# Five buffers for gathered rows instead of three in the last stage of a 46,509-instruction block kernel

## The chip, the cores and the metric

The kernel runs on one core of a Trainium2 chip. TensorE (PE) multiplies, VectorE (DVE) and ScalarE (ACT) work elementwise, GpSimd (POOL) does some elementwise work and issues the indirect transfers (gathers), SyncE (SP) issues the plain transfers. The engines run side by side, each in its own fixed order. The metric is the device time of one execution in microseconds (us).

## The reference

Two transformer blocks over 256 tokens of width 2048, in float32. The stage that is changed is the last: the second half of a feed-forward layer with a lookup (PEER). Each token has 8 x 16 = 128 chosen experts out of 16,384, each with a weight; the layer's output is the weighted sum of the experts' rows of `peer_v`. A residual is added, and a last norm is applied.

```python
a = einsum('cd,ced->ce', xc, u[ic])            # stage U: token times chosen rows of peer_u
w = gelu(a) * gate
y = einsum('ce,ced->cd', w, v[ic])             # stage V: weighted sum of chosen rows of peer_v
x = x + y
out = rms_norm_2(x, g_final)
```

## The kernel before, in words

The two tables (16,384 rows of 2048 columns each) are worked on in two ways. For the first columns (`GU` = 640 of `peer_u`, `GV` = 512 of `peer_v`) the chosen rows are gathered, one per token: a gather fetches 128 rows, the s-th expert of 128 tokens. For the other columns the whole table is streamed and multiplied densely, with a matrix of weights `L` (tokens by experts, zero where an expert was not chosen).

Stage V runs over 128 blocks of 128 experts. In a block, SP loads three raw tiles of 128 x 512 (`vraw`, six slots). Each is split for TensorE into a high and a low part: ScalarE writes `vh` (L210), VectorE writes `vl` (L212), six slots each. The weights are split in the same way (`wh`, `wl`), once per two blocks. Then TensorE makes 18 matmuls of 128 x 512, three (L1520, L1525, L1526) for each of three column groups `n` and two token halves `tt`, into six accumulators `va`.

Beside it run 256 gathers (2 token halves times 128 slots) of 128 x 512 into tiles `gt`. `gather` (L1261) has GpSimd issue the indirect transfer, and `add` (L1473) has VectorE multiply the gathered rows by their weight and add them into `y` (L1474). A list `flying` holds up to three gathers; a new one goes into the buffer that the oldest add has freed. Each block takes `n` adds, the rest divided by the blocks left up to 126:

```python
n = -(-left // max(NE - 2 - i, 1)) if i else 0
```

Two loads of residual rows (`load_y`) and the five parts of the last norm's vector (`gfin`) are queued on SP behind the last raw tile of blocks 1, 16 and 24. In the last two blocks the matmuls are ordered by hand: those of block 126 are held back and then sorted by token half, so that the first half's accumulators are done while the second half's are still worked on; the first half's norm runs beside them. After the last matmul come the final sums, the norm's products (GpSimd mostly), the scaling and the stores.

The order of each engine's work is laid out ahead of time by a planner that goes through the program in order of priority, with its own costs for each instruction; `keep_in_program_order` keeps an add behind all VectorE work that was written before it, while work written later may be moved ahead of it. Tiles of a pool with one tag share its slots, and an instruction that would write to a slot waits until the earlier readers are done.

Stage U, ahead of V, has the same shape: gathers of 128 x 640 with five buffers (four of `BASE`, one of `EXTRA`) beside a streamed part whose raw tiles hold 704 KB.

Of the kernel before, what the change touches and what calls it, by code (L numbers as in the profile page):

```python
# [12 lines left out]
F32 = mybir.dt.float32  # L13
F32R = mybir.dt.float32r
# [6 lines left out]
P = 128  # L21
T = 256
NT = 2
D = 2048
KD = D // P
W = 512
DFF = 8192
EPS = 1e-6
GU = 640
GV = 512  # L30
# [23 lines left out]
def tile_conv_mlp_then_attention_peer(ctx, tc, a, out):  # L54
    nc = tc.nc
    PSUM = bass.MemoryType.PSUM
# [643 lines left out]
    with ExitStack() as pc:  # L700
# [310 lines left out]
        with ExitStack() as pj:  # L1011
# [6 lines left out]
            for n, src in enumerate((so, lo_)):  # L1018
                c = 0
# [47 lines left out]
    NE = 128  # L1067
# [144 lines left out]
    ready = []  # L1212
# [45 lines left out]
    EXTRA = {"gt": 1, "u": 1}  # L1258
    UNITS = [(k, min(4, KU - k)) for k in range(0, KU, 4)]

    def gather(pool, bufs, w, table, tt, s):  # L1261
        gt = pool.tile([P, w], F32, name="gt", tag="gt", bufs=bufs)
        nc.gpsimd.indirect_dma_start(  # L1263
            out=gt, out_offset=None, in_=table,
            in_offset=bass.IndirectOffsetOnAxis(ap=e4[:, tt, s:s + 1], axis=0),
        )
        return gt, tt, s
# [18 lines left out]
    for i in range(NE):  # L1286
        if i == len(HALVES):
            eb_ctx.close()
            own["gt"] = us_ctx.enter_context(tc.tile_pool(name="ug", bufs=2))
        if more is None and not bg.items and "gt" in own:  # L1290
            rt_ctx.close()
            rt_ctx = ExitStack()
            more = rt_ctx.enter_context(tc.tile_pool(name="more", bufs=2, side=side))
        if i % 2 == 0:
            aps = psa.tile([P, 2, T], F32, name="aps", tag="acc")
        if i in HALVES:
            ready_parts = []
            for n in range(2):
                t = (us, eb)[i % 2].tile([P, KU, P], F32, name="ue", tag="uraw")
                nc.sync.dma_start(  # L1300
                    t.rearrange("p k e -> p (k e)"),
                    pre.done[i][n].rearrange("p k e -> p (k e)"),
                )
                ready_parts.append(t.bitcast(F32R))
        else:
            raw = us.tile([P, DU], F32, name="uraw", tag="uraw")
            if i in pre.done:
                nc.sync.dma_start(raw, pre.done[i][0].rearrange("p k e -> p (k e)"))
                rawt = raw.rearrange("p (k e) -> p k e", k=KU)
            else:  # L1310
                nc.sync.dma_start(raw, a["peer_u_2"][0, i * P:(i + 1) * P, GU:D])
                rawp = raw.rearrange("p (j k) -> p k j", k=KU)
        for k0, nk in UNITS:
            if i in HALVES:
                hi_k = [ready_parts[0][:, k0 + kk, :] for kk in range(nk)]
                lo_k = [ready_parts[1][:, k0 + kk, :] for kk in range(nk)]
            else:
                pool = ring("u")
                nb = EXTRA["u"] if pool is more else BASE["u"]
                uh = pool.tile([P, 4, P], F32R, name="uh", tag="uh", bufs=nb)  # L1320
                ul = pool.tile([P, 4, P], F32R, name="ul", tag="ul", bufs=nb)
                if i in pre.done:
                    split(uh[:, :nk], ul[:, :nk], rawt[:, k0:k0 + nk])
                else:
                    with tc.high_priority(offset=EARLY):
                        ut = pst.tile([P, 4, P], F32, name="tp_u", tag="tr")
                        for kk in range(nk):
                            nc.tensor.transpose(ut[:, kk, :], rawp[:, k0 + kk, :], ident)  # L1328
                    split(uh[:, :nk], ul[:, :nk], ut[:, :nk])
                hi_k = [uh[:, kk, :] for kk in range(nk)]  # L1330
                lo_k = [ul[:, kk, :] for kk in range(nk)]
            for kk in range(nk):
                k = k0 + kk
                s0, s1 = k == 0, k == KU - 1
                o = aps[:, i % 2, :]
                nc.tensor.matmul(o, lhsT=hi_k[kk], rhs=xbh[:, k, :], start=s0, stop=False)  # L1336
                nc.tensor.matmul(o, lhsT=hi_k[kk], rhs=xbl[:, k, :], start=False, stop=False)  # L1337
                nc.tensor.matmul(o, lhsT=lo_k[kk], rhs=xbh[:, k, :], start=False, stop=s1)  # L1338
            bg.pump(1)
        if i % 2 == 1:  # L1340
            nc.scalar.activation(
                L[:, :, i - 1:i + 1], aps.rearrange("p i t -> p t i"), AF.Copy
            )
        n = min(len(ready) + len(flying), -(-left // (NE - i))) if more is not None else 0
        for _ in range(n):
            while ready and len(flying) < BASE["gt"] + EXTRA["gt"]:
                pool = ring("gt")
                nb = EXTRA["gt"] if pool is more else BASE["gt"]
                flying.append(gather(pool, nb, GU, u4, *ready.pop(0)))
            dot(*flying.pop(0))  # L1350
        left -= n
    us_ctx.close()
# [99 lines left out]
    ps_ctx.close()  # L1452


    with tc.tile_pool(name="psv", bufs=1, space=PSUM) as psv, tc.tile_pool(name="vs", bufs=2) as vs:
        NV = DN // W
        H = W // 2
        ys = [
            xb_pool.tile([P, D + W + H], F32, name=f"y{tt}", tag=("xbh", "xbl")[tt]) for tt in range(NT)
        ]  # L1460
        gl = vs.tile([P, W], F32, name="gl", bufs=1)
        gfin = [
            (0, W, ys[0][:, D:D + W]), (W, 2 * W, ys[1][:, D:D + W]), (2 * W, 3 * W, gl),
            (3 * W, 3 * W + H, ys[0][:, D + W:]), (3 * W + H, D, ys[1][:, D + W:]),
        ]

        def load_y(lo, hi):
            for tt in range(NT):
# [4 lines left out]
        def add(gt, tt, s):  # L1473
            tc.keep_in_program_order(nc.vector.scalar_tensor_tensor(  # L1474
                ys[tt][:, 0:GV], gt, wtok[:, tt, s:s + 1], ys[tt][:, 0:GV], ALU.mult, ALU.add
            ))

        vslots = [(tt, s) for tt in range(NT) for s in range(SL)]
        left = len(vslots)
        for i in range(NE):  # L1480
# [6 lines left out]
                    split(wh[:, :, ts], wl[:, :, ts], L[:, ts, i:i + 2].rearrange("p t i -> p i t"))  # L1487
            vhl = []
            for n in range(NV):
                raw = vr.tile([P, W], F32, name="vraw", tag="vraw")  # L1490
                fetch = nc.sync.dma_start(
                    raw, a["peer_v_2"][0, i * P:(i + 1) * P, GV + n * W:GV + (n + 1) * W]
                )
                vh = vs.tile([P, W], F32R, name="vh", tag="vh", bufs=6)
                vl = vs.tile([P, W], F32R, name="vl", tag="vl", bufs=6)
                op = split(vh, vl, raw)
                vhl.append((vh, vl))
            with tc.issue_after(fetch.ins):
                if i == 1:
                    load_y(0, GV)  # L1500
                elif i == 16:
                    load_y(GV, D)
                elif i == 24:
                    for lo, hi, g_ in gfin:
                        nc.sync.dma_start(g_, bcast_row(a["g_final_2"][lo:hi], hi - lo))
            if i == 8:
# [4 lines left out]
            if i == 0:  # L1511
                todo.sort(key=lambda c: c[2])
            if i == NE - 2:
                held, todo = todo, []
            elif i == NE - 1:
                todo = sorted(held + todo, key=lambda c: (c[2], c[1], c[0]))
            for e, n, tt, (vh, vl) in todo:
# [6 lines left out]
                    tc.keep_in_program_order(op)  # L1524
                nc.tensor.matmul(acc[tt][n], lhsT=wh[:, e % 2, tk], rhs=vl, start=False, stop=False)  # L1525
                nc.tensor.matmul(acc[tt][n], lhsT=wl[:, e % 2, tk], rhs=vh, start=False, stop=s1)  # L1526
            n = -(-left // max(NE - 2 - i, 1)) if i else 0
            for _ in range(min(n, left)):
                while vslots and len(flying) < 3:
                    flying.append(gather(vs, 3, GV, v4, *vslots.pop(0)))  # L1530
                add(*flying.pop(0))
                left -= 1

        for tt in range(NT):
            y = ys[tt]
            part = sm.tile([P, 4], F32, name="fp", tag="ssq4")
            for c in range(4):
                cs = slice(c * W, (c + 1) * W)
                if c:
                    nc.vector.tensor_tensor(y[:, cs], acc[tt][c - 1], y[:, cs], ALU.add)  # L1540
                junk = vs.tile([P, W], F32, name="fj", tag="gt", bufs=3)
                nc.scalar.activation(junk, y[:, cs], AF.Square, accum_out=part[:, c:c + 1])
                mul = nc.vector if (tt, c) == (1, 3) else nc.gpsimd
                for lo, hi, g_ in gfin:
                    if c * W <= lo < (c + 1) * W:
                        mul.tensor_tensor(y[:, lo:hi], y[:, lo:hi], g_, ALU.mult)
            ssq = sm.tile([P, 1], F32, name="fssq", tag="ssq")
            nc.vector.tensor_reduce(ssq, part, AX.X, ALU.add)
            rr, _ = rms_scale(ssq, D, f"fin{tt}")
            w = 2 * W if tt == 0 else W  # L1550
            for c in range(D // w):
                cs = slice(c * w, (c + 1) * w)
                if tt == 1 and c % 2:
                    nc.scalar.activation(y[:, cs], y[:, cs], AF.Copy, scale=rr)
                else:
                    nc.vector.tensor_scalar(y[:, cs], y[:, cs], rr, None, ALU.mult)
                nc.sync.dma_start(out[0, tt * P:(tt + 1) * P, cs], y[:, cs])
# [18 lines left out]
```

## Time and profile before

| | |
|---|---|
| median of 3 runs | 3219.36 us (3219.32 to 3228.66) |
| the profiled execution | 3219.82 us |
| its span in the profile | 3218.1 us |
| mean granted TensorE clock | 0.989 of full |
| TensorE, VectorE, ScalarE, GpSimd busy | 3067.6, 2382.2, 1573.3, 862.3 us |
| data moved | 799.51 MB, mean 248 GB/s |
| stage V, first to last matmul starts | 2600.0 to 3204.6 us |

Times in the rows are in us from the span's start unless marked ns. A group's row gives the line, the engine, the operation, the tiles written and read, and the count. Idle time is put down to what ended it. Matmuls are pipelined, so their busy times overlap. The chain of waits is followed back from the last instruction, at each step to what released it.

### The profile page before, as it was taken

The page shows a single profiled execution, that of the slowest core. Times are in us where ns is not written, and L with a number is a line of the kernel's source. Part 1 is how long each engine was busy: PE and PEld are TensorE (multiplying, and loading weights), DVE is VectorE, ACT ScalarE, POOL GpSimd, SP SyncE. Part 2 cuts the span into 40 slices and gives each one's busy share as a digit, 9 for nine tenths or more (in the row PEclk, how much of TensorE's full clock was granted, in tenths as well). Part 3 has the DMA queues.
Part 4 walks back from the last instruction along what each step waited for, and adds up shares of the span by engine and source line. Part 5 has one row for each costly group of instructions (what it writes and reads, how often), then busy time and mean ns, then how long its engine had stood idle before and what let it go on. Part 6 is the DMA issues. An engine that isn't in the chain of part 4 may idle for free.

```text
span 3218.1 us, 46509 instructions
## 1 busy us (share of the span) xinstructions
PE 3067.6 (95%) x16266; PEld 2571.2 (80%) x16266; DVE 2382.2 (74%) x4415; ACT 1573.3 (49%) x2574; POOL 862.3 (27%) x823
## 2 busy tenths in 40 slices
PE   8889999999999999999999989999999998889997
PEld 7668777787888877777788889999998976667775
DVE  6987677666777765455777977776777977778887
ACT  7555555444454465545445223334443564445554
POOL 1640000000000000000000016654444964555554
PEclk9999999999999999999999999999999999999999
DMA  6445599998999844445997479998886358888886
GB/s 212 134 167 185 179 298 314 317 300 257 306 312 314 265 156 154 157 163 170 318 300 254 160 248 323 333 313 288 283 287 209 122 196 296 279 269 293 293 281 233
DMA packets 334502, 799.51 MB, mean 248 GB/s; under 512 B 29143, under 2 KB 67002, under 8 KB 334010
## 3 DMA queue, kind: packets, MB, share of 16 engines
q1 hardware_dynamic: 273744, 574.82, 54.7%
q0 software_dynamic: 52192, 207.26, 19.0%
q10 hardware_dynamic: 8330, 14.44, 1.3%
q8 instruction: 128, 2.10, 0.3%
q14 instruction: 108, 0.88, 0.1%
HBM read 731.66 MB, written 64.75 MB: 247 GB/s over the span
## 4 chain that ended last, share of the span: by engine, by line
PE 59%; DMA 21%; DVE 9%; issue 8%; POOL 2%; ACT 1%; SPq 0%; DVEq 0%; ACTq 0%; POOLq 0%
PE acc L378 13%; PE acc L379 13%; PE acc L380 13%; DMA gt<-peer_v,e 12%; PE aps L1338 4%; PE aps L1336 4%; PE aps L1337 4%; DVE gc L522 2%; PE tp_u L1328 2%; PE ep L1406 2%; PE wp L1437 1%; DVE lo L212 1%; POOL gt L1263 1%; DVE y L1474 1%; DMA uraw<-peer_u 1%
## 5 line engine op out<-in xcount | busy, mean ns | idle before, releaser
L212 DVE TENSOR_TENSOR lo<-raw,hi 128x1024 fp32r<-128x1024 f32 (+2 forms) x580 | 707.5, 1229 | 361.2 <-ACT hi L210 359.5
L210 ACT ACTIVATE hi<-raw 128x1024 fp32r<-128x1024 f32 (+2 forms) x580 | 605.0, 1049 | 559.4 <-PE acc L380 432.1
L379 PE MATMUL acc<-lo,xbh 128*128 128x512 f32 (+1 forms) x1034 | 414.6, 401 | 15.2 <-DVE lo L212 15.1
L380 PE MATMUL acc<-hi,xbl 128*128 128x512 f32 (+1 forms) x1034 | 412.8, 400 | 0.0
L378 PE MATMUL acc<-hi,xbh 128*128 128x512 f32 (+1 forms) x1034 | 409.0, 400 | 0.9 <-ACT hi L210 0.9
L1263 POOL DMA_INDIRECT gt<-peer_u,e x256 | 282.6, 1104 | 467.8 <-DVE gt L1270 206.7
L1263 POOL DMA_INDIRECT gt<-peer_v,e x256 | 305.6, 1194 | 290.5 <-DVE y L1474 255.7
L210 ACT ACTIVATE vh<-vraw 128x512 fp32r<-128x512 f32 x384 | 239.6, 633 | 289.0 <-DMA vraw<-peer_v 233.0
L1338 PE MATMUL aps<-xbh,ul 128*128 128x256 f32 x1254 | 365.1, 291 | 5.8 <-DVE ul L212 5.6
L1336 PE MATMUL aps<-xbh,uh 128*128 128x256 f32 x1254 | 363.1, 290 | 0.0
L1337 PE MATMUL aps<-xbl,uh 128*128 128x256 f32 x1254 | 360.8, 288 | 0.0
L1525 PE MATMUL va<-vl,wh 128*128 128x512 f32 x768 | 313.1, 408 | 46.7 <-DVE vl L212 45.9
L1526 PE MATMUL va<-vh,wl 128*128 128x512 f32 x768 | 300.9, 392 | 0.0
L1520 PE MATMUL va<-vh,wh 128*128 128x512 f32 x768 | 297.7, 393 | 2.7 <-ACT vh L210 2.6
L1474 DVE SCALAR_TENSOR_TENSOR y<-gt,wtok,y 128x512 f32<-128x512 f32 x256 | 191.9, 749 | 115.2 <-DMA gt<-peer_v,e 113.7
L212 DVE TENSOR_TENSOR vl<-vraw,vh 128x512 fp32r<-128x512 f32 x384 | 255.9, 685 | 4.6 <-ACT vh L210 4.6
L1338 PEld LDWEIGHTS aps<-xbh,ul 128*128 128x128 f32 x1254 | 241.1, 192 | 10.8 <-DVE ul L212 10.7
L379 PEld LDWEIGHTS acc<-lo,xbh 128*128 128x128 f32 x1034 | 196.5, 190 | 66.4 <-DVE lo L212 20.9
L1336 PEld LDWEIGHTS aps<-xbh,uh 128*128 128x128 f32 x1254 | 241.0, 192 | 0.6
L1337 PEld LDWEIGHTS aps<-xbl,uh 128*128 128x128 f32 x1254 | 240.9, 192 | 0.0
L1525 PEld LDWEIGHTS va<-vl,wh 128*128 128x128 f32 x768 | 144.8, 188 | 119.7 <-DVE vl L212 91.6
L378 PEld LDWEIGHTS acc<-hi,xbh 128*128 128x128 f32 x1034 | 196.8, 190 | 48.2 <-ACT hi L210 2.1
(549 smaller groups left out, 6297.0 us busy)
## 6 DMA issues: line engine op xcount, KB each, us to landing
vraw<-peer_v SPq DMA_DIRECT2D x384, 256.0 KB, 4.8
raw<-w_in SPq DMA_DIRECT2D x88, 1024.0 KB, 5.0
raw<-w_up SPq DMA_DIRECT2D x64, 1024.0 KB, 8.2
raw<-w_down SPq DMA_DIRECT2D x64, 1024.0 KB, 7.1
uraw<-peer_u SPq DMA_DIRECT2D x64, 704.0 KB, 5.7
uraw<-ud SPq DMA_DIRECT2D x50, 704.0 KB, 5.8
tq<-peer_u SPq DMA_DIRECT2D x152, 176.0 KB, 7.3
ud<-tu POOLq DMA_DIRECT2D x38, 704.0 KB, 6.7
```

The source lines that it names most:

```text
L210: op = nc.scalar.activation(hi, src, AF.Copy, scale=scale)
L212: nc.vector.tensor_tensor(lo, src, hi, ALU.subtract)
L378: nc.tensor.matmul(o, lhsT=xh_, rhs=hi, start=s0, stop=False)
L379: nc.tensor.matmul(o, lhsT=xh_, rhs=lo, start=False, stop=False)
L380: nc.tensor.matmul(o, lhsT=xl_, rhs=hi, start=False, stop=s1)
L1263: nc.gpsimd.indirect_dma_start(out=gt, out_offset=None, in_=table, in_offset=bass.IndirectOffsetOnAxis(ap=e4[:, tt, s:s + 1], axis=0),)
L1336: nc.tensor.matmul(o, lhsT=hi_k[kk], rhs=xbh[:, k, :], start=s0, stop=False)
L1337: nc.tensor.matmul(o, lhsT=hi_k[kk], rhs=xbl[:, k, :], start=False, stop=False)
L1338: nc.tensor.matmul(o, lhsT=lo_k[kk], rhs=xbh[:, k, :], start=False, stop=s1)
L1520: op = nc.tensor.matmul(acc[tt][n], lhsT=wh[:, e % 2, tk], rhs=vh, start=s0, stop=False)
L1525: nc.tensor.matmul(acc[tt][n], lhsT=wh[:, e % 2, tk], rhs=vl, start=False, stop=False)
L1526: nc.tensor.matmul(acc[tt][n], lhsT=wl[:, e % 2, tk], rhs=vh, start=False, stop=s1)
```

## The change

Five things in stage V. (1) The gathers go into five tiles `gts`, used in turn by hand, instead of three slots of a tag; up to five fly. (2) The raw tiles get a seventh slot, in a pool of its own; the split tiles have five slots each instead of six. (3) The adds are spread over the blocks up to 120 instead of 126. (4) The last norm's vector is loaded at block 123 (`NE - 5`) instead of 24; its third part goes into the first gather tile instead of a tile of its own, and the scratch tile of the norm's squares takes three of the gather tiles in turn. (5) Of block 126 only the matmuls of column groups 1 and 2 are held back for the last block; those of group 0 run at once.

```diff
-    def gather(pool, bufs, w, table, tt, s):
-        gt = pool.tile([P, w], F32, name="gt", tag="gt", bufs=bufs)
+    def gather(gt, table, tt, s):
...
-                flying.append(gather(pool, nb, GU, u4, *ready.pop(0)))
+                gt = pool.tile([P, GU], F32, name="gt", tag="gt", bufs=nb)
+                flying.append(gather(gt, u4, *ready.pop(0)))
...
-    with tc.tile_pool(name="psv", bufs=1, space=PSUM) as psv, tc.tile_pool(name="vs", bufs=2) as vs:
+    with tc.tile_pool(name="psv", bufs=1, space=PSUM) as psv, ExitStack() as vs_ctx:
+        vs = vs_ctx.enter_context(tc.tile_pool(name="vs", bufs=2))
...
-        gl = vs.tile([P, W], F32, name="gl", bufs=1)
+        gts = [vs.tile([P, GV], F32, name=f"gt{n}", bufs=1) for n in range(5)]
         gfin = [
-            (0, W, ys[0][:, D:D + W]), (W, 2 * W, ys[1][:, D:D + W]), (2 * W, 3 * W, gl),
+            (0, W, ys[0][:, D:D + W]), (W, 2 * W, ys[1][:, D:D + W]), (2 * W, 3 * W, gts[0]),
             (3 * W, 3 * W + H, ys[0][:, D + W:]), (3 * W + H, D, ys[1][:, D + W:]),
         ]
+        gnext = 0
...
+        v2 = vs_ctx.enter_context(tc.tile_pool(name="v2", bufs=1))
+        vturn = 0
...
-                raw = vr.tile([P, W], F32, name="vraw", tag="vraw")
+                raw = (vr if vturn % 7 < 6 else v2).tile([P, W], F32, name="vraw", tag="vraw")
+                vturn += 1
...
-                vh = vs.tile([P, W], F32R, name="vh", tag="vh", bufs=6)
-                vl = vs.tile([P, W], F32R, name="vl", tag="vl", bufs=6)
+                vh = vs.tile([P, W], F32R, name="vh", tag="vh", bufs=5)
+                vl = vs.tile([P, W], F32R, name="vl", tag="vl", bufs=5)
...
-                elif i == 24:
+                elif i == NE - 5:
                     for lo, hi, g_ in gfin:
                         nc.sync.dma_start(g_, bcast_row(a["g_final_2"][lo:hi], hi - lo))
...
             if i == NE - 2:
-                held, todo = todo, []
+                held = [c for c in todo if c[1]]
+                todo = [c for c in todo if not c[1]]
...
-            n = -(-left // max(NE - 2 - i, 1)) if i else 0
+            n = -(-left // max(NE - 8 - i, 1)) if i else 0
             for _ in range(min(n, left)):
-                while vslots and len(flying) < 3:
-                    flying.append(gather(vs, 3, GV, v4, *vslots.pop(0)))
+                while vslots and len(flying) < len(gts):
+                    flying.append(gather(gts[gnext], v4, *vslots.pop(0)))
+                    gnext = (gnext + 1) % len(gts)
                 add(*flying.pop(0))
                 left -= 1
...
-                junk = vs.tile([P, W], F32, name="fj", tag="gt", bufs=3)
+                junk = gts[1 + c % 3]
```

## Rows read from the trace of the kernel before

**Rows 1.** the page's chain that ended last, share of the span by line

```profile
PE acc L378 13%; PE acc L379 13%; PE acc L380 13%; DMA gt<-peer_v,e 12%; PE aps L1338 4%; PE aps L1336 4%; PE aps L1337 4%; DVE gc L522 2%; PE tp_u L1328 2%; PE ep L1406 2%; PE wp L1437 1%; DVE lo L212 1%; POOL gt L1263 1%; DVE y L1474 1%; 
```

**Rows 2.** matmuls into va in stage V: duration min/median/max ns, first and last start

```profile
L1520 PE MATMUL va<-vh,wh x768: 387/389/632, 2600.0 to 3204.1; 128*128 128x512 f32 x192
...
L1526 PE MATMUL va<-vh,wl x768: 387/389/632, 2601.1 to 3204.6; 128*128 128x512 f32 x192
```

**Rows 3.** TensorE at the end of stage V, first and last of 25

```profile
3199.09 0.40 PE L1526 MATMUL va<-vh,wl 128*128 128x512 f32 x1
...
3204.55 0.39 PE L1526 MATMUL va<-vh,wl 128*128 128x512 f32 x1
```

**Rows 4.** stage V: us, PE, PEld, DVE, ACT, POOL, PEclk, DMA share, GB/s

```profile
2600.00:3205.00 605.00, 557.56 (x2304) 424.91 (x2304) 481.89 (x714) 307.76 (x464) 310.93 (x261) 0.99 0.85 280
```

**Rows 5.** the chain of waits from 2580 us on, by line

```profile
by line: DMA gt<-peer_v,e 58.8%; issue 13.5%; DVE y L1474 6.5%; DVE vl L212 4.5%; DMA vraw<-peer_v 3.4%; POOL gt L1263 3.1%; PE va L1525 1.5%; PE va L1526 1.3%; PE va L1520 1.2%; PE wp L1437 1.0%; DVE wl L212 0.9%; PE ep L1406 0.6%; ACT vh 
```

**Rows 6.** waits in stage V: engine, line, waited for: us in total, times, longest

```profile
ACT vh L210 <- DMA vraw<-peer_v: 233.0, 197, 6.3
DVE y L1474 <- DMA gt<-peer_v,e: 113.7, 126, 3.6
...
PE va L1525 <- DVE vl L212: 45.9, 61, 2.6
ACT vh L210 <- PE va L1526: 23.1, 18, 3.8
```

**Rows 7.** timeline of stage V: start, us, engine, line, operation [idle before <-releaser]

```profile
2942.27 1.15 POOL L1263 DMA_INDIRECT gt<-peer_v,e  x1 [0.71 <-DVE y L1474]
...
2949.00 1.29 DVE L212 TENSOR_TENSOR vl<-vraw,vh 128x512 fp32r<-128x512 f32 x2
...
2949.35 1.15 POOL L1263 DMA_INDIRECT gt<-peer_v,e  x1 [1.01 <-DVE y L1474]
...
2950.20 0.75 DVE L1474 SCALAR_TENSOR_TENSOR y<-gt,wtok,y 128x512 f32<-128x512 f32 x1
...
2950.87 0.69 DVE L212 TENSOR_TENSOR vl<-vraw,vh 128x512 fp32r<-128x512 f32 x1
...
2952.91 1.07 DVE L212 TENSOR_TENSOR wl<-L,wh 128x512 fp32r<-128x512 f32 x1
...
2953.89 0.68 DVE L212 TENSOR_TENSOR vl<-vraw,vh 128x512 fp32r<-128x512 f32 x1
```

**Rows 8.** the adds in stage V: duration ns, first and last start

```profile
L1474 DVE SCALAR_TENSOR_TENSOR y<-gt,wtok,y x256: 731/751/757, 2603.6 to 3194.7; 128x512 f32<-128x512 f32 x128
```

**Rows 9.** DMA of stage V: packets, MB, share; KB each, median to landing

```profile
q1 hardware_dynamic: 55584, 102.00, 50.3%
q0 software_dynamic: 20480, 67.13, 34.3%
...
gt<-peer_v,e POOLq DMA_INDIRECT x256, 5.5
y<-res_d SPq DMA_DIRECT2D x2, 768.0 KB, 8.9
```

**Rows 10.** a stretch of stage U, columns as in rows 4

```profile
1940.00:2140.00 200.00, 194.23 (x1547) 188.63 (x1547) 157.74 (x347) 73.50 (x139) 122.80 (x114) 1.00 0.93 333
```

**Rows 11.** DMA issues in that stretch, columns as in rows 9

```profile
uraw<-peer_u SPq DMA_DIRECT2D x22, 704.0 KB, 6.9
uraw<-ud SPq DMA_DIRECT2D x17, 704.0 KB, 6.0
gt<-peer_u,e POOLq DMA_INDIRECT x114, 6.5
```

**Rows 12.** transfers of raw tiles in stage V

```profile
DMA to landing us min/median/max: 2.5/4.8/8.1
```

**Rows 13.** VectorE in the tail

```profile
3206.59 1.00 DVE L176 TENSOR_TENSOR rms_y<-rms_y,rms_t 128x1 f32<-128x1 f32 x1
```

## The prediction

> **What bounds the kernel now.** I read the page first. Its chain of waits is mostly TensorE in the projections, but one transfer has 12% of the span, the gathered rows of peer_v [rows 1]. They belong to the last stage, V, which the change alone touches, so the rest is read there. V runs from its first matmul at 2600.0 us to its last at 3204.55 + 0.39 = 3204.9 us [rows 2, 3], 604.9 us, and in it no engine is full: VectorE is busy 482 of 605 us, GpSimd 311, ScalarE 308, the DMA engines 0.85 [rows 4]. TensorE's 558 us are pipelined matmuls that overlap, so I use its dense pace: from 3199.09 to 3204.55 us 24 matmuls start, 0.2275 us each [rows 3]. All 2304 would take 524 us, and a block (18) 4.10. TensorE therefore lacks work for about 80 us.
>
> What it lacks is split rows, and what those lack stands in the chain of V: 58.8% is "gather lands", 3.4% raw rows [rows 5]. The waits give it in time: VectorE stands 113.7 us in 126 waits for a gather at the add (L1474), and TensorE 45.9 us for the low half of a split, which VectorE makes [rows 6]. VectorE is in order: while it stands at an add, the splits behind it wait, raw slots stay taken, ScalarE waits for raw rows (233 us), and TensorE runs dry. So the wait for raw rows is mostly a result.
>
> Why is a gather late? There are three buffers. GpSimd issues one at 2942.27; when it has landed, its add frees the buffer, and the gather three further on, into the same buffer, goes out at 2949.35 [rows 7]. 7.08 us for three is 2.36 us per row, and 256 such are 604 us: the stage's length. The adds do take from 2603.6 to 3194.7 us, 2.31 us each [rows 8]. V runs at the pace of the gather loop.
>
> **The change, part by part.** Costs per block at full pace, for the next bounds:
> - TensorE: 4.10 us.
> - VectorE, by starts of neighbours [rows 7]: a split 0.605 (two end after 1.29, one alone is 0.685), an add 0.67, a weight split 0.98, one per two blocks. With two adds 1.815 + 0.49 + 1.34 = 3.65 us, with three 4.32, with none 2.31.
> - DMA: the two data queues took 50.3 + 34.3% of 16 engines for 606 us to move 169.1 MB [rows 9], so full engines need 3.03 us per MB. Three raw tiles (0.786 MB) and two gathers (0.524) take 3.97 us, with three gathers 4.77, with none 2.38.
>
> *Five gather buffers.* The loop becomes five per turn. If the turn stays 7.08 us, that is 1.42 us a gather; the nearest row for a fuller DMA is the U stage with its five buffers: 114 gathers in 200 us, 1.75 us each, of 2.5 KB rows [rows 10, 11]. Those are the ends; at two adds per block they ask for 2.8 to 3.5 us, under TensorE's 4.10, so the loop ceases to bind there. GpSimd's own 1.15 us per issue [rows 7], 2.3 to 3.5 us per block, hides beside it.
>
> A rule of the Trainium skill speaks against this part. The profile's median from issue to landing is 5.5 us [rows 9]. "DMA: Bandwidth & Descriptors", section Anatomy of one DMA, gives about 2.0 us fixed and bytes/436 GB/s beside it, which for 256 KB is an estimated 2.6 us. By it the old loop would turn in some 4.2 us (the trace's 7.08 less 5.5, and 2.6), three buffers would give a row per 1.4 us, and this part would be worth nothing; the 126 waits say otherwise.
>
> *Adds finish six blocks earlier.* The divisor goes from 126 - i to 120 - i. Worked through the loop: before, 6 blocks have three adds and 119 have two; after, blocks 1 to 18 have three, 19 to 119 two, the last eight none. The first 18 blocks thus ask for 4.77 us of DMA, and 4.25 to 5.25 of the gather loop (three times the ends above): they are slower than TensorE. I take the DMA at the share 0.96, between the U stage's 0.93 [rows 10] and full: 4.97 us.
>
> *Seven raw slots.* A raw slot's turn is landing (median 4.8 us [rows 12]) plus some 2.5 us of issue, split and queue, against 7 x 1.365 = 9.6 us of TensorE time for seven tiles. It gives 1.4 us more cover; by itself zero, it keeps a fuller DMA from showing.
>
> *Five split slots.* One tile less ahead, 1.37 us. ScalarE stood 18 times because all were full [rows 6], at most 18 x 1.37 = 25 us; at least nothing, since four tiles (5.5 us) still lie ahead. It matters only where VectorE is late too, which is 61 of the 768 matmuls that take it [rows 2, 6], 8%: 2 us.
>
> *The last norm's vector.* Its five loads (1.05 MB, 3.2 us of DMA) move from block 24, where DMA is wanted, to block 123, where no gather runs. In SP's queue they stand behind that block's raw load and ahead of the later ones; one goes into the first gather buffer, which the last gather also uses. Its add belongs to block 119, and that raw load already waits for a split of block 121, so SP should stop nowhere: zero. If the add were late, SP would hold the raw rows of four blocks for that time, some 2 us. The 3.2 us are inside the bounds per block.
>
> *Holding two of three column groups.* Block 126's first group is now multiplied at once, so only five tiles need be held. The last token half keeps 15 matmuls rather than 18, 0.7 us less cover for the first half's norm. Against it, the first column's products on GpSimd are done early; in the trace, the last of its 1.3 us products lie beside VectorE's tiny norm steps, which take 1.00 us and delay the final sums [rows 13]. Between -1.3 and +0.7: -0.5 us.
>
> **The sum for V.** Block 0: 4.1. 18 blocks at 4.97: 89.5. The residual rows at block 16, 1.57 MB [rows 9], DMA-bound: 5.0. 101 blocks: TensorE and DMA are 4.10 and 3.97, so close that they disturb one another; the U stage in that state kept TensorE busy 194.2 of 200 us [rows 10], 0.97: 4.22 each, 426.2. Eight at 4.10: 32.8. Split slots: 2. Together 559.6, that is 45.3 less than 604.9; with the tail 45.8. The profiled run took 3219.8 us (span 3218.1), the runs' median 3219.4, so they are one: **3174 us**.
>
> Range: with full engines, 18 at 4.77 and 109 at TensorE's pace, V is 542 us (3156); nothing but TensorE, 524 (3139). With a DMA share of 0.90, blocks at 5.30 and 4.41, it is 583 (3198); with the split slots at half their worst about 3210. I put 3148 to 3208.
>
> **The rivals.**
> - *Raw rows become late: slower.* V's transfers share engines that are 0.85 busy; two more gathers in flight stand before each raw tile. If the raw slot's turn exceeds 7 x 604.9 / 384 = 11.0 us, V is slower than before; with 2.5 us around it, that means landing over 8.5 us, where now it is 4.8 at the median and 8.1 at most [rows 12]. At 9 us, 11.5 / 7 = 1.64 us per tile: 631 us, 3246. Against it: in the U stage five gathers fly beside 704 KB tiles and these land in 6 to 6.9 us [rows 11]. The Trainium skill's front page, "Trainium Kernel Development and Optimization", Key Constraints, says the same of the engines: all queues run on the same 16 and interleave. The share in this trace leaves 15% to interleave into. 7 in 100.
> - *Gathers slow in proportion.* If the gather path itself gives 2.3 us per row whatever the depth, five in flight take 11.8 us each and V stays: 3219. The U stage's 1.75 us for larger rows [rows 11] speaks against it. With it goes the case that the loop does not bind at all and VectorE stands at the adds for another reason, which also leaves 3219; the turn of 7.08 us, which gives the stage's length by itself, speaks against that. Together 8 in 100. The rule on the fixed cost, above, would make it this case.
> - *DMA holds it short.* Share near 0.90 or the first 18 blocks at the loop's worst: 3190 to 3210, about 3200; 20 in 100. Before, the share in V was 0.85 [rows 4], which speaks for it.
> - *TensorE alone.* DMA and VectorE leave no gaps: below 3156, about 3148. VectorE's 3.65 of 4.10 us leaves little slack; 10 in 100.
>
> The forecast itself (3156 to 3190) has 55 in 100. A measurement of this kernel tells 0.3%, 9.7 us, from no change. Faster by more takes the forecast, the short case and TensorE alone: 0.85; same 0.08; slower 0.07.
>
> **What would show it.** After: the waits of the add for gathers fall from 113.7 us to under 40, mostly in the first 18 blocks, which should take some 90 us; the chain of V leaves the gather for TensorE and splits; the DMA share in the middle is 0.93 to 0.97; gathers land in 6 to 7 us and raw rows in 5 to 6.5; the last matmul stands near 3159 us; GpSimd issues its last gather some 40 us before that. The prediction is wrong if raw rows land over 8.5 us, if the order that the planner gives VectorE puts adds ahead of splits that TensorE needs, or if SP stands at the vector's loads.

## The result, and the profile after

The changed kernel takes 3142.1 us (median of 6 runs, 3134.8 to 3156.9) against 3221.6 us for the kernel before on the same chips: 0.9751 of it, 95% interval 0.9731 to 0.9771. The gain of 79.5 us is well over the forecast 45, and the time lies 6 us below the stated range.

The profiled execution has a span of 3142.2 us, 75.9 less than before. Its first and last groups of V's matmuls (columns as in [rows 2]):

```profile
L1526 PE MATMUL va<-vh,wh x768: 387/389/794, 2601.9 to 3128.0; 128*128 128x512 f32 x192
...
L1532 PE MATMUL va<-vh,wl x768: 388/389/628, 2603.4 to 3128.5; 128*128 128x512 f32 x192
```

V runs from 2601.9 to 3128.5 + 0.4 = 3128.9 us, 527.0 us instead of 604.9. It begins 1.9 us later, and from its end to the span's end there are 13.3 us, before 13.2. So -77.9 + 1.9 + 0.1 = -75.9: all of it is V.

The chain of V, by line, which [rows 5] shows for before:

```profile
by line: PE va L1531 19.9%; PE va L1526 19.9%; PE va L1532 19.8%; issue 9.5%; POOL gt L1262 6.4%; DMA gt<-peer_v,e 5.8%; DMA vraw<-peer_v 5.3%; DVE y L1476 2.7%; DVE vl L212 2.5%; PE wp L1437 1.2%; PE ep L1406 1.0%; ACT oj L1428 0.8%; DVE w
```

Three shares of 20% are TensorE's own matmuls; the gather's landing has gone from 58.8% to 5.8%. The waits, as in [rows 6]:

```profile
ACT vh L210 <- PE va L1532: 153.6, 195, 3.1
...
ACT vh L210 <- DMA vraw<-peer_v: 18.7, 23, 1.9
...
DVE y L1476 <- DMA gt<-peer_v,e: 7.7, 7, 4.0
...
PE va L1531 <- DVE vl L212: 1.6, 1, 1.6
```

They have turned round. TensorE waits 1.6 us for a low half (45.9 before), the add 7.7 us for gathers (113.7). ScalarE now waits for TensorE to free a split slot, 153.6 us: the queue ahead of TensorE is full. Raw rows, 233 us of waiting before, are at 18.7. The seventh slot is not what did that: with five gather tiles and six raw slots (below) they are at 32.8, which bears out that most of that wait was a result of VectorE's stops.

V in stretches of 40 us (columns as in [rows 4]):

```profile
2600.00:2640.00 40.00, 38.13 (x162) 31.39 (x163) 35.92 (x54) 26.72 (x42) 27.02 (x23) 0.96 0.95 319
2640.00:2680.00 40.00, 39.55 (x174) 32.19 (x173) 35.95 (x55) 21.64 (x33) 24.85 (x23) 1.00 1.00 363
2680.00:2720.00 40.00, 40.00 (x178) 32.95 (x177) 38.34 (x59) 23.44 (x36) 26.60 (x22) 1.00 0.98 337
...
2800.00:2840.00 40.00, 38.41 (x170) 31.50 (x169) 35.53 (x54) 22.32 (x33) 31.63 (x22) 1.00 0.95 319
2840.00:2880.00 40.00, 40.00 (x178) 33.14 (x177) 39.80 (x61) 23.92 (x35) 30.09 (x25) 1.00 1.01 363
...
2960.00:3000.00 40.00, 40.00 (x178) 33.10 (x178) 36.92 (x55) 23.44 (x35) 23.95 (x21) 1.00 0.95 321
```

At TensorE's dense pace 40 us hold 176 matmuls, and those that overlap an edge are counted too, so 178 is a stretch without a gap. Only the first two and the sixth fall short. The DMA share is 0.95 to 1.01 up to 3080 us, where the gathers end.

The two data queues and the issues (columns as in [rows 9]):

```profile
q1 hardware_dynamic: 55728, 102.26, 55.3%
q0 software_dynamic: 20480, 67.13, 37.4%
...
vraw<-peer_v SPq DMA_DIRECT2D x378, 256.0 KB, 5.3
gt<-peer_v,e POOLq DMA_INDIRECT x256, 6.0
```

Gathers land in 6.0 us at the median (5.5 before), raw rows in 5.3 (4.8).

### The profile page after: what moved, and what is told of

It is laid out like the page before. It is cut to its first block, busy times and chain, and to the rows that moved or that the text cites. A ratio compares the mean times of both kernels' runs of the same rounds, so it can differ in the third digit from the quotient of the medians.

```text
span 3142.2 us, 46502 instructions
## 1 busy us (share of the span) xinstructions
PE 3034.4 (97%) x16266; PEld 2575.7 (82%) x16266; DVE 2380.8 (76%) x4415; ACT 1570.3 (50%) x2574; POOL 870.8 (28%) x823
## 4 chain that ended last, share of the span: by engine, by line
PE 71%; DMA 11%; DVE 8%; issue 6%; POOL 2%; ACT 2%; SPq 0%; ACTq 0%; POOLq 0%; DVEq 0%
PE acc L378 13%; PE acc L379 13%; PE acc L380 13%; PE aps L1337 4%; PE aps L1335 4%; PE aps L1336 4%; PE va L1531 4%; PE va L1526 4%; PE va L1532 4%; DMA uraw<-peer_u 2%; DVE gc L522 2%; PE tp_u L1327 2%; POOL gt L1262 2%; PE ep L1406 2%; PE wp L1437 1%
## 5 line engine op out<-in xcount | busy, mean ns | idle before, releaser
L1262 POOL DMA_INDIRECT gt<-peer_v,e x256 | 321.0, 1254 | 169.4 <-DVE y L1476 111.4
L210 ACT ACTIVATE vh<-vraw 128x512 fp32r<-128x512 f32 x384 | 236.1, 632 | 191.7 <-PE va L1532 153.6
L1531 PE MATMUL va<-vl,wh 128*128 128x512 f32 x768 | 299.3, 390 | 1.6 <-DVE vl L212 1.6
L380 PEld LDWEIGHTS acc<-hi,xbl 128*128 128x128 f32 x1034 | 195.7, 189 | 46.1 <-issue 2.3
L1526 PE MATMUL va<-vh,wh 128*128 128x512 f32 x768 | 226.5, 391 | 2.5 <-ACT vh L210 2.5
L1269 DVE SCALAR_TENSOR_TENSOR gt<-gt,xg 128x640 f32<-128x640 f32 x256 | 203.3, 820 | 21.0 <-DMA gt<-peer_u,e 20.4
```

What stands on the lines that cost most here:

```text
L210: op = nc.scalar.activation(hi, src, AF.Copy, scale=scale)
L380: nc.tensor.matmul(o, lhsT=xl_, rhs=hi, start=False, stop=s1)
L1262: nc.gpsimd.indirect_dma_start(out=gt, out_offset=None, in_=table, in_offset=bass.IndirectOffsetOnAxis(ap=e4[:, tt, s:s + 1], axis=0),)
L1526: op = nc.tensor.matmul(acc[tt][n], lhsT=wh[:, e % 2, tk], rhs=vh, start=s0, stop=False)
```

## The experiments

All are variants of the changed kernel. The chips differ by some 20 us, so each has the ratio to the kernel before on its own chip, and the length of V in its one profiled execution (first matmul to last). The changed kernel: 0.9751 and 527.0 us, and in a second measurement below 0.9743 and 524.6, so V differs by 2.4 us between two executions of one kernel.

**Three gather tiles.**

```diff
-        gts = [vs.tile([P, GV], F32, name=f"gt{n}", bufs=1) for n in range(5)]
+        gts = [vs.tile([P, GV], F32, name=f"gt{n}", bufs=1) for n in range(3)]
...
-                junk = gts[1 + c % 3]
+                junk = vs.tile([P, W], F32, name="fj", tag="fj", bufs=2)
```

> The changed kernel with three gather tiles again, all else kept. If the gather loop was the bound (7.1 us for three rows, some 7.5 with the fuller queues), 256 adds take 605 to 640 us and the kernel about 3215 to 3250 us. If the raw slots, the later vector or the spread of the adds brought the gain, it stays near 3142.

Measured: 1.0089 (1.0059 to 1.0118), as much as 3250 us on the chips of the result, V 634.8 us. The whole gain is gone, and a little more. The adds, and who waits up to 3130 us (as in [rows 8] and [rows 6]):

```profile
L1476 DVE SCALAR_TENSOR_TENSOR y<-gt,wtok,y x256: 732/751/764, 2625.4 to 3218.4; 128x512 f32<-128x512 f32 x128
```

```profile
DVE y L1476 <- DMA gt<-peer_v,e: 106.6, 104, 3.4
...
PE va L1531 <- DVE vl L212: 57.0, 66, 2.2
```

To the end of V the two waits come to 132.9 and 67.3 us (113.7 and 45.9 before). The adds take 593.0 us, 2.32 each, as in the kernel before and a little under the 605 expected, although seven raw slots and all other parts of the change are there. Since they must end at block 120 now, the eight blocks left come on top: from the last add at 3218.4 to the end of the last matmul at 3251.7 are 33.3 us, eight times 4.16, where the kernel before has 10.2. With three tiles the earlier end of the adds thus makes up 23 of the 30 us by which V is longer than before; another 5 are a later first add.

**Four gather tiles.** The same line with `range(4)`.

> Four gather tiles. By the loop, 7.1 to 7.6 us for four is 1.8 to 1.9 us a row, 454 to 486 us for 256, below TensorE's 524: 3142 to 3155 us. If the pace is simply in proportion to the tiles, or the planner's order asks for more, it lands half way, near 3170.

Measured: 0.9763 (0.9741 to 0.9784), V 539.3 us. The loop's arithmetic holds: four are nearly enough. The add still waits 31 us for gathers in the profile; whether the fifth tile is worth the 12 us that V shows is not settled by the times, whose interval overlaps with the changed kernel's.

**Five gather tiles alone.** The change pays for them with the sixth split slots, so this keeps what pays for them.

```diff
-                raw = (vr if vturn % 7 < 6 else v2).tile([P, W], F32, name="vraw", tag="vraw")
+                raw = vr.tile([P, W], F32, name="vraw", tag="vraw")
...
-            (0, W, ys[0][:, D:D + W]), (W, 2 * W, ys[1][:, D:D + W]), (2 * W, 3 * W, gts[0]),
+            (0, W, ys[0][:, D:D + W]), (W, 2 * W, ys[1][:, D:D + W]), (2 * W, 3 * W, gl),
...
-                elif i == NE - 5:
+                elif i == 24:
...
-            n = -(-left // max(NE - 8 - i, 1)) if i else 0
+            n = -(-left // max(NE - 2 - i, 1)) if i else 0
```

> The kernel before with five gather tiles alone, and what makes room for them (five split slots, one column group of block 126 not held back); six raw slots, adds up to block 126, the vector at block 24. If the loop is the whole cause: 3140 to 3150 us. If the seventh raw slot is needed beside it, raw rows are waited for again: 3160 to 3185.

Measured: 0.9758 (0.9738 to 0.9779), V 535.4 us. The gather tiles, with the five split slots and the group of block 126 that isn't held back, bring practically all of the gain in time, and 69.5 of the 77.9 us of V. No add waits for a gather any more, and raw rows are waited for (as in [rows 6], up to 3130 us):

```profile
ACT vh L210 <- DMA vraw<-peer_v: 32.8, 32, 4.9
```

**Six raw slots.** Only the first edit of the five gather tiles alone, the one above.

> The changed kernel with six raw slots instead of seven. If raw rows land in 5 to 6 us, a slot's turn of about 8 us is just the 8.2 us that TensorE takes for six tiles: 3142 to 3152 us. If the seventh slot carries part of the gain: 3160 or more.

Measured: 0.9774 (0.9748 to 0.9799), V 540.0 us; the interval overlaps with the changed kernel's, so it was run again beside it (below).

**Adds up to block 126.** Only the last edit of the five gather tiles alone. The gathers that come after block 123 overwrite the third part of the norm's vector in the tile that they share, so columns 1024 to 1535 are scaled with the wrong gain; the instructions are the same.

> The changed kernel with the adds spread up to block 126 as before. If TensorE alone sets the pace, 3140 to 3147 us. If ending the adds early is part of the gain (the last blocks free of gathers, the first column's norm early), 3150 or more.

Measured: 0.9754 (0.9727 to 0.9781), V 529.0 us: no difference. The early end of the adds brings no time; it makes the shared tile possible.

**Three adds in each of the first 18 blocks, enforced.** The planner may move splits of later blocks ahead of an add. This forbids it in blocks 2 to 19:

```diff
-                op = split(vh, vl, raw)
+                op = nc.scalar.activation(vh, raw, AF.Copy)
+                low = nc.vector.tensor_tensor(vl, raw, vh, ALU.subtract)
+                if 2 <= i <= 19:
+                    tc.keep_in_program_order(low)
```

> The changed kernel with VectorE's splits of blocks 2 to 19 held behind the adds written before them, so that the first 18 blocks really take three adds each. If the forecast failed because the planner had spread the adds, this brings back its term of 9 to 16 us: 3151 to 3160 us. If DMA and gathers were simply fast enough for three per block, 3142.

Measured: 0.9839 (0.9812 to 0.9865), V 554.1 us, 27 more than the changed kernel. The first theory has the direction, and its size is too small. V's first 160 us in four stretches (columns as in [rows 4]):

```profile
2618.80:2658.80 40.00, 35.09 (x137) 27.68 (x138) 32.53 (x49) 19.38 (x30) 23.83 (x21) 0.91 0.83 274
2658.80:2698.80 40.00, 32.10 (x125) 25.21 (x124) 30.13 (x45) 17.70 (x26) 23.43 (x22) 0.91 0.87 284
2698.80:2738.80 40.00, 32.28 (x131) 25.23 (x130) 31.73 (x46) 16.74 (x26) 22.03 (x20) 0.96 0.86 298
2738.80:2778.80 40.00, 40.00 (x178) 33.08 (x177) 38.90 (x59) 24.51 (x37) 28.90 (x23) 1.00 1.00 352
```

All of the loss is in the first 120 us, and the DMA share there is 0.83 to 0.87: it isn't the DMA that holds these blocks, as the forecast had it. VectorE's timeline shows what does (time, us, engine, line, operation, idle before and what ended it):

```profile
2662.68 1.10 DVE L212 TENSOR_TENSOR wl<-L,wh 128x512 fp32r<-128x512 f32 x1 [0.64 <-PE va L1535]
2663.70 1.53 DVE L1476 SCALAR_TENSOR_TENSOR y<-gt,wtok,y 128x512 f32<-128x512 f32 x2
2665.90 0.75 DVE L1476 SCALAR_TENSOR_TENSOR y<-gt,wtok,y 128x512 f32<-128x512 f32 x1 [0.68 <-DMA gt<-peer_v,e]
2667.35 0.75 DVE L1476 SCALAR_TENSOR_TENSOR y<-gt,wtok,y 128x512 f32<-128x512 f32 x1 [0.70 <-DMA gt<-peer_v,e]
2668.01 3.13 DVE L1502 TENSOR_TENSOR vl<-vraw,vh 128x512 fp32r<-128x512 f32 x5
```

Four adds now stand in a row. The third and fourth find their gathers not landed, and five splits that TensorE needs stand behind them. That the gathers are late because their tiles were freed and refilled in a bunch is an argument, not shown by a run. Nor are the gathers the whole of it; the waits up to 2740 us (as in [rows 6]):

```profile
PE va L1534 <- DVE vl L1502: 20.2, 9, 3.6
...
DVE wl L212 <- ACT wh L210: 12.7, 7, 2.9
DVE y L1476 <- DMA gt<-peer_v,e: 10.1, 10, 2.3
```

VectorE stands 12.7 us for the high half of the weights and 10.1 us for gathers, and the held splits wait through both; TensorE waits 20.2 us for them. After such gaps the granted clock falls too, to a mean of 0.91, 0.91 and 0.96 of the upper level in the three stretches (0.96 and 1.00 in the first two of the changed kernel); that can be at most (0.09 + 0.09 + 0.04) x 40 = 8.8 us of the loss.

**The same hold on blocks 80 to 97,** where the loop gives two adds per block.

> The control: the same hold on blocks 80 to 97, where each block has two adds and none are behind. Both theories: 3139 to 3146 us. If holding the order costs by itself, it shows here.

Measured: 0.9750 (0.9726 to 0.9775), V 526.8 us. The hold costs nothing by itself.

**Two matmuls instead of three.** The product of the weights' low part and the rows' high part is left out, so the output is less exact.

```diff
-                nc.tensor.matmul(acc[tt][n], lhsT=wh[:, e % 2, tk], rhs=vl, start=False, stop=False)
-                nc.tensor.matmul(acc[tt][n], lhsT=wl[:, e % 2, tk], rhs=vh, start=False, stop=s1)
+                nc.tensor.matmul(acc[tt][n], lhsT=wh[:, e % 2, tk], rhs=vl, start=False, stop=s1)
```

> The changed kernel without the third matmul of each split (low weights by high rows), so that the output is less exact; TensorE's part of V falls from 524 to 349 us. It shows the next limit. If that is the DMA at 2.9 us per MB, V takes 495 to 515 us and the kernel 3110 to 3130. If it is VectorE at its dense pace, 467 us, about 3085 to 3100. If gathers or raw slots hold V near its present length in any case, 3140.

Measured: 0.9673 (0.9636 to 0.9710), V 490.4 us. A third less work for TensorE shortens V by only 37 us: the next limits are close. One stretch, and the queues (columns as in [rows 4] and [rows 9]):

```profile
2800.00:2900.00 100.00, 88.09 (x319) 53.27 (x317) 97.24 (x147) 59.98 (x92) 71.21 (x55) 1.00 1.00 352
2900.00:3000.00 100.00, 88.16 (x319) 53.19 (x317) 97.59 (x148) 59.53 (x92) 71.59 (x56) 1.00 0.99 348
```

```profile
q1 hardware_dynamic: 56003, 103.31, 58.1%
q0 software_dynamic: 20480, 67.13, 36.7%
```

The DMA share is 1.00 and VectorE is busy 97%, so both stand at their ends together, and neither theory is singled out. From 2600 to 3110 us the queues move 170.4 MB in 0.948 of 510 us, 2.84 us per MB of full engines.

**The changed kernel, six raw slots, and adds written evenly.** Four on one chip. The even spread gives two adds to most blocks and a third to one in six or seven:

```diff
-            n = -(-left // max(NE - 8 - i, 1)) if i else 0
+            n = min(i, NE - 9) * 256 // (NE - 9) - max(min(i, NE - 9) - 1, 0) * 256 // (NE - 9) if 0 < i < NE - 8 else 0
```

> The changed kernel as it is, beside the others on one chip, 0.975 of the kernel before. V 527 us, TensorE without gaps but for 3 to 5 us.

> Six raw slots, as in the earlier run, whose V took 540 us with all of the loss in its first 200 us. If the seventh slot carries part of the gain, 8 to 13 us slower than the changed kernel on this chip; if that was chance, the same within 3 us.

> The changed kernel with the adds written evenly, 256 over 119 blocks, two and now and then three, instead of three in each of the first 18. If TensorE's pace is all that is left, a gain of 0 to 5 us (the gaps in V's first 80 us and at its middle); if the order of the adds costs more than the trace shows, more.

> Both: even adds and six raw slots. If the seventh raw slot is wanted only because the first blocks take more adds than TensorE's time allows transfers for, V falls from 540 to some 527 to 530 us and the kernel equals the changed one. If six slots are too few for the fuller DMA in any case, it stays 8 to 13 us slower.

| | ratio | interval | V, us |
|---|---|---|---|
| changed kernel | 0.9743 | 0.9718 to 0.9768 | 524.6 |
| six raw slots | 0.9785 | 0.9766 to 0.9803 | 538.5 |
| even adds | 0.9756 | 0.9732 to 0.9780 | 527.0 |
| even adds, six raw slots | 0.9745 | 0.9719 to 0.9771 | 526.7 |

Six slots lose 14 us of V, as in their first run (13), and 0.4% of the time; the intervals just touch. With even adds the six slots lose nothing. V's first 200 us with six slots, adds as in the change and then even:

```profile
2594.50:2794.50 200.00, 194.82 (x814) 150.60 (x815) 179.94 (x268) 106.98 (x165) 124.86 (x109) 0.99 0.95 327
```

```profile
2591.30:2791.30 200.00, 198.25 (x864) 163.21 (x865) 185.26 (x276) 117.19 (x174) 128.34 (x105) 0.99 0.97 334
```

814 matmuls against 864. So the seventh slot is wanted for the beginning of V, where the loop writes three adds per block, and for nothing else that these runs show. Even adds bring no gain where seven slots are there. No variant that does all of the work beats the changed kernel beyond the measurement.

## Why the prediction was wrong

**What was right.** The cause: V ran at the pace of the gather loop. Three tiles bring back 2.32 us per add and all of the time; five alone take nearly all of it away. Most signs came as listed: the add's waits under 40 us (7.7), gathers landing in 6 to 7 us (6.0) and raw rows in 5 to 6.5 (5.3), a DMA share around 0.96, the last gather some 40 us before the last matmul (3084.1 us, 45 before). Two did not: the beginning of V did not take some 90 us, and the last matmul stands at 3128.5 us, not near 3159. Raw rows did not become late (5.3 us at the median and 8.4 at most, where over 8.5 were needed), and gathers did not slow in proportion. The five split slots cost nothing that TensorE's 1.6 us of waits would show. The vector's loads go out from 3099.3 to 3101.8 us, and the raw rows behind them follow at 3101.9. The tail's -0.5 is +0.1.

**The step that failed** is the term for the first 18 blocks: that they ask for three adds each and are slower than TensorE, at 4.97 us each, with 5.0 us for the residual rows. For block 0, the 18 and these rows the sum had 98.6 us. The changed kernel takes 80.1 for its first 19 blocks (from its first matmul to its 343rd): 18.5 of the 32.6 us by which V came out shorter than the sum. Adds in stretches of 40 us (time, VectorE busy and count):

```profile
2600.00:2640.00 40.00, 13.52 (x18) 0.00 (x0) 0.00 (x0) 0.96 0.95 319
2640.00:2680.00 40.00, 16.34 (x22) 0.00 (x0) 0.00 (x0) 1.00 1.00 363
2680.00:2720.00 40.00, 15.89 (x22) 0.00 (x0) 0.00 (x0) 1.00 0.98 337
2720.00:2760.00 40.00, 16.73 (x23) 0.00 (x0) 0.00 (x0) 1.00 0.97 348
```

85 adds stand beside the 692 matmuls of the same stretches, 38 blocks: 2.2 per block, not three. I read adds per block from the loop, but the planner lays out VectorE's order, and it may put later splits ahead of an add; why it does so where it does is not shown. In VectorE's order in the trace the 48th add stands behind the splits of 22 whole blocks and more, where the loop's text has it in block 16. The hold on blocks 2 to 19 shows that the term is real when the order is as I took it, and then larger: the first 19 blocks take 106.5 us. The hold's DMA share of some 0.85 shows that I had also put it down to the wrong thing. The prediction did name the planner's order as a risk, but the other way round: adds ahead of splits. That adds drift behind could be read before: in the old kernel's order the 18th add, which its loop writes in block 6, stands behind the splits of 10 blocks.

**Two smaller terms.** The 101 blocks at 4.22 took 527.0 - 80.1 - 32.8 = 414.1 us, 4.10 each, TensorE's own pace: 12.1 us. The factor 0.97 was borrowed from the U stage; with TensorE and DMA both near full, V shows no such loss. And 2 us for the split slots, in the same 414.1. Behind them lies a price that was too high: 3.03 us per MB came from busy shares at 0.85. After, the same reckoning gives (0.553 + 0.374) x 531 us / 169.4 MB = 2.91, and in the run with two matmuls 2.84. Two adds per block are then 3.7 to 3.8 us of DMA beside TensorE's 4.10, which leaves room where I saw none. The seventh raw slot, put at nothing by itself, is worth 13 to 14 us of V with the adds as the loop writes them, and nothing with even adds.

The rule on the fixed cost of a transfer (the Trainium skill, "DMA: Bandwidth & Descriptors", Anatomy of one DMA) would have made the gather tiles worthless. This trace doesn't agree in the loaded state: a gather lands after 6.0 us, not the estimated 2.6.

**The outcome was the rival "TensorE alone",** which had 10 in 100 and stood at about 3148; its 524 us of matmuls are met within 3 us. The prediction's own figure for nothing but TensorE was 3139 us, 3 below the measured time, and the stated range began at 3148, above it.

**What stays open.** Whether the fifth tile gains over four, and which of VectorE and DMA would be next. The five split slots and the group that isn't held back were in every run, so neither was priced alone. Why the loss in V's first 80 us varies (some 3 us) was not tried.

## What to carry to other kernels

Where a loop of few buffers sets the pace, its turn divided by the buffers, times the count, gives the stage's length, and a stage that matches it to 1%, as this one did, can be expected to follow the buffer count until the next engine's dense pace. Take that engine's pace as the forecast, and charge the work of a stretch by what the trace shows it to do there, counted in instructions per stretch, not by where the program's text puts it. A busy share at part load is no price: here it overstated what full engines paid, 3.03 us per MB against 2.84.

## What the runs showed of the hardware

The time that packets hold the DMA engines fell per byte as the engines filled: 3.03 us per MB at a share of 0.85, 2.91 in the changed kernel (0.93), 2.84 in the run with two matmuls (0.95 as a mean, 0.99 to 1.00 in its middle), all with the same 2 KB rows. Why it fell is not shown. And the median time from issue to landing of raw rows and gathers rose only from 4.8 to 5.3 and from 5.5 to 6.0 us while V's mean rate went from 280 to 320 GB/s.
